# Matmul and batch norm on one core: the first tiles' scale and shift spread without TensorE, and a third chunk of them by columns

## The chip, the cores and the metric

The kernel runs on one core of a Trainium2 chip. The metric is the device time of one execution in microseconds (us); a lower one is better. A core has TensorE (PE; its weight loads are PEld), VectorE (DVE), ScalarE (ACT), GpSimd (POOL) and SyncE (SP), which here issues DMAs alone. Every engine runs its own list of instructions in order and waits for others by semaphores. Matmuls write into PSUM, 8 banks of 128 x 512 float32.

## The reference

```python
y = np.matmul(x, weight)                      # x [16, 512, 1024], weight [1024, 768]
mean = np.mean(y, axis=(0, 1), keepdims=True)
var = np.var(y, axis=(0, 1), keepdims=True)
y_norm = (y - mean) / np.sqrt(var + eps)
return (gamma * y_norm + beta).astype(np.float32)
```

All is float32 outside; the kernel multiplies in bfloat16. Every output column needs the mean and variance over all 8192 rows before its first element can be stored.

## The kernel before

The 8192 rows are 16 chunks of 512 (CH), the 768 columns 6 tiles of 128. GpSimd's DMAs load x (L403) and the weight; VectorE turns x into xT_sb (L428, L435). TensorE then makes y in two forms.

**By columns** (tiles 2 to 5, line L575): the weight stands still, and y comes with columns on the partitions. VectorE takes statistics (L711; for most of tile 2 ScalarE does, L720 and L724), ScalarE keeps y as bfloat16 (L715). Scale and shift are then one value a partition, but the normalized tile must be turned back into rows, by TensorE transposes (L1044), or by SP's DMA transposes (L1220 and L1106).

**By rows** (tiles 0 and 1 together, GA = 2, NA = 256 columns): for chunks 0 to 13 (RC = C - 2 = 14) x stands still (L510), and y comes with rows on the partitions, as it is stored. ScalarE squares (L659), VectorE adds to sums (L662), GpSimd or VectorE adds the squares (L666), ScalarE keeps y (L672). Here scale and shift vary along the free axis, so every partition needs both rows of 256 values. For chunks 14 and 15 these two tiles go by columns instead (`ga_unit`, L814, with statistics in L821 and keeping in L827).

When all chunks are in, `sums_rows` (L871) multiplies the sums with a vector of ones on TensorE, `aggregate_rows` (L887) joins them with the statistics of the column chunks, `root_rows` takes the root, and `scale_rows` and `shift_rows` give scale and shift, a value a partition. `spread_rows` puts them on all partitions: `spread` (L903) multiplies a broadcast column with the float32 identity, once for each tile and for scale and shift, into two PSUM banks; `shift_sbuf` (L915) copies the shift to SBUF for GpSimd.

`rows_out` then writes a row chunk: VectorE multiplies (L937), VectorE (for the k in ADDED) or GpSimd adds the shift (L942), SP stores (L946). `ga_block` writes a column chunk: VectorE normalizes two tiles (L1064), TensorE turns eight blocks (L1074), ScalarE copies (L1082), SP stores (L1085).

`raw_spread` does a spread without TensorE already, for parts of tiles 2 to 4: VectorE copies and transposes in 32 x 32 blocks (L1141, L1142), then copies of 32 partitions gather the values into one row and deal it to the four groups of 32 partitions (L1145), and ScalarE copies them to PSUM (L1158).

The order of all this is not written out. Each piece is a `Task` with a due time, engines with assumed durations, what it depends on and the buffers that it takes. `arrange` (L122) goes through the tasks as a list scheduler and fixes each engine's order from those durations: among the tasks that could begin within 0.2 us (`look`) of the first, the one that is due earliest. So a task that is added or changed can move all that follows on every engine. Transposes can be put between the matmuls of a column unit (`hosts`). `banks`, `rings` and others model PSUM banks and SBUF space.

The last tile (5) ends the kernel: its statistics, `affine` (L1324), norms (L1348), transposes (L1044), copies (L1361) and stores (L1364).

Of the kernel before, what the change touches and what calls it, by code (L numbers as in the profile page):

```python
# [227 lines left out]
def kernel(  # L228
# [19 lines left out]
    P = 128  # L248
    NT = N // P
    KQ = K // 4  # L250
    CH = 512
# [13 lines left out]
    GA = 2  # L265
    NA = GA * P
    GY = 2
    PAD = 50
    HELD = 1
    PAIRED = 1  # L270
    ASTAT = {2:tuple(range(4,16))}
    RC = C - 2
    XT, YB, SQ = C - EARLY, 28, 3
    ADDED = (0,6,16,28,40)
    PARTED, LATE, SINGLE = (4,5,7,8,9,10), (12,13,14,15), (2,3,6)
# [17 lines left out]
    def seq(bi):  # L293

        ins = bi.ins
        prev = last.get(ins.engine)
        if prev is not None:
            tc.add_manual_dep(
                ins, prev,
                mybir.DependencyInfo(mybir.DependencyClass.NoSync, mybir.DependencyReason.DATA),  # L300
                reason="order",
            )
        last[ins.engine] = ins.name
        return bi
# [26 lines left out]
        seq(nc.vector.memset(sums[nt][:, 1:2], float(len(ASTAT[nt]) * CH)))  # L331
    msq = singles.tile([P, GA], f32)
    gst = singles.tile([P, GA, 3 + 12 * (C - RC)], f32)
    seq(nc.vector.memset(gst, float(RC * CH)))
    ngamma = singles.tile([P, NT], f32)
    nscale = singles.tile([P, 1], f32)
# [522 lines left out]


    S = clock[0]
    tot_slot, a0_slot, a1_slot = Slot(banks), Slot(banks), Slot(banks)
    aff = {}

    def sums_rows(eng):
# [24 lines left out]
    def root_rows(eng):  # L890
        seq(nc.scalar.activation(std[:, g], mv[:, g, 1], AF.Sqrt, bias=eps_sb, scale=1.0))

    def scale_rows(eng):
        seq(nc.vector.reciprocal(std[:, g], std[:, g]))
        seq(nc.vector.tensor_mul(scale[:, g], std[:, g], gamma_sb[:, g]))

    def shift_rows(eng):
        seq(nc.vector.tensor_mul(tmp[:, g], mv[:, g, 0], scale[:, g]))
        seq(nc.vector.tensor_sub(shift[:, g], beta_sb[:, g], tmp[:, g]))

    def spread(dst, row, nt):

        seq(nc.tensor.matmul(dst, row[:, nt:nt + 1].to_broadcast([P, P]), ident32, start=True, stop=True,  # L903
                             skip_group_check=True))

    def spread_rows(i):
        def emit(eng):
            a_ps = psum.tile([P, CH], f32, tag="b")
            aff[i] = a_ps[:, 0:NA]
            for a in range(GA):  # L910
                spread(a_ps[:, a * P:(a + 1) * P], (scale, shift)[i], a)
        return emit

    def shift_sbuf(eng):
        seq(nc.scalar.copy(sum1[:, 0:NA], aff[1]))  # L915

    U = S - 30.0
    s1 = task(U, pe(0.9), sums_rows, merges, takes=[tot_slot])
    se = task(U, dve(0.8), sums_entry, [s1], True, uses=[tot_slot])
    ag = [task(U, dve(0.25), aggregate_rows(a), [se] + [h[0] for k, h in ga_half.items() if k[0] == a]) for a in range(GA)]  # L920
    rt = task(U, {"ACT": (0.2, 0.3)}, root_rows, ag)
    sc = task(U, dve(0.3), scale_rows, [rt], True)
    sr = task(U + 0.1, dve(0.35), shift_rows, [sc], True)
    p0 = task(U, pe(0.45), spread_rows(0), [sc], takes=[a0_slot])
    p1 = task(U, pe(0.45), spread_rows(1), [sr], takes=[a1_slot])
    p1.look = 0.6
    sh = task(U, act(0.3), shift_sbuf, [p1], uses=[a1_slot])


    def rows_out(c, s0, s1, k):  # L930
        due = S + 5.0 + 0.62 * k
        n = s1 - s0
        slot = Slot(rings, n * NA)

        def norm(eng):
            slot.o = piece(slot).rearrange("p (s n) -> p s n", n=NA)
            seq(nc.vector.tensor_mul(  # L937
                slot.o, y_row[c].y[:, s0:s1], aff[0][:, None, :].to_broadcast([P, n, NA])))

        def add(eng):  # L940
            row = sum1[:, 0:NA] if eng == "POOL" else aff[1]
# [8 lines left out]
        a = task(due, dve(0.3 * n), norm, [p0] + keeps, takes=[slot], uses=[y_row[c], a0_slot])  # L950
        b = task(due + 0.4, dve(0.3 * n) if k in ADDED else pool(0.59 * n), add, [a, p1 if k in ADDED else sh],
                 uses=[slot, a1_slot] if k in ADDED else [slot])
# [103 lines left out]
    def ga_block(c, due):  # L1056
        yslot = y_row[c]
        slot, bank = Slot(rings, RT * NA), Slot(banks)
        todo = []

        def norm_ga(a):
            def emit(eng):
                part = yslot.y[:, a]
                seq(nc.vector.tensor_scalar(  # L1064
                    part, part, scale[:, a:a + 1], shift[:, a:a + 1], op0=ALU.mult, op1=ALU.add))
            return emit

        def step():
            if not todo:
                o_ps = psum.tile([P, RT, GA, P], bf16, tag="b")  # L1070
                bank.tile = o_ps
                todo.extend((o_ps[:, s, a], yslot.y[:, a, s * P:(s + 1) * P]) for s in range(RT) for a in range(GA))
            dst, src = todo.pop(0)
            seq(nc.tensor.transpose(dst, src, ident))  # L1074

        def emit(eng):
            for _ in range(emit.task.count):
                step()

        def copy(eng):  # L1080
            slot.o = piece(slot).rearrange("p (s n) -> p s n", n=NA)
            seq(nc.scalar.copy(slot.o, bank.tile.rearrange("p s a n -> p s (a n)")))  # L1082

        def store(eng):
            seq(nc.sync.dma_start(out_flat[c * CH:(c + 1) * CH, 0:NA].rearrange("(s p) n -> p s n", p=P), slot.o))  # L1085

        emit.step = step
        norms = [task(due, dve(0.25), norm_ga(a), [sr] + [h[1] for k, h in ga_half.items() if k[1] == c], True, uses=[yslot])
                 for a in range(GA)]
        t = task(due, pe(0.0555 * RT * GA), emit, norms, takes=[bank], uses=[yslot])  # L1090
        emit.task = t
        turns[t] = [RT * GA, RT * GA]
        d = task(due, act(0.905), copy, [t], takes=[slot], uses=[bank])
        task(due, {"SP": (0.38, 0.4)}, store, [d], dma=RT * NA * P * 4 / 1024 / 365.0 * 1.024, uses=[slot])

    for c in range(RC, C):
        ga_block(c, S - 29.8 + 35.5 * (c - RC))

    def raw_turn(nt, c, due):

# [26 lines left out]
    def raw_spread(nt, fin_task):  # L1127
        bank = Slot(banks)
        k = sorted(RAW).index(nt)
        acc, at = ((sum2, 0), (sum2, 2 * P), (sum3, 2 * P))[k]  # L1130
        row = acc[:, at:at + 2 * P].rearrange("p (i n) -> p i n", n=P)
        wide, turned = sum1[:, NA + 64 * k:NA + 64 * (k + 1)], sum3[:, 64 * k:64 * (k + 1)]
# [279 lines left out]
```

## Time and profile before

| | us |
|---|---|
| median of 3 runs (range) | 205.81 (205.71 to 205.83) |
| span of the profiled execution | 204.07 |
| median less span | 1.74 |
| PE busy / DVE / ACT / POOL | 189.3 / 159.3 / 146.2 / 124.1 |
| last matmul of a statistic ends | 186.62 |
| first scaled rows (L937) begin | 107.59 |
| first store of output issued | 109.10 |

For the profiled execution only its span is given; what lies around it is taken from the runs. Times in the profile count from the first instruction. A group's line gives file line, engine, operation, output and inputs with their shapes, count, busy time and mean duration. The chain of work that ended last is followed back from the end, step by step, to what released each piece. In the tables by stretch each engine has its busy time and, in brackets, its instructions; then come the granted clock of TensorE, the DMA engines' busy share and GB/s.

### The profile page before, as it was taken

Reading aid. Unit: us, or ns where it says so; the run is one execution under the profiler, and the core shown is the slowest. Engines: PE = TensorE matmul, PEld = TensorE weight load, DVE = VectorE, ACT = ScalarE, POOL = GpSimd, SP = SyncE. Lnnn points to the kernel's source line nnn. Section 1 sums busy time; section 2 is a strip of 40 time slices with the busy share of each in tenths; the row PEclk is TensorE's granted clock in tenths of the full one; section 3 lists DMA queues with packets and bytes.
Section 4 is the critical chain, followed back from the end, with each engine's and each line's share of the span. In section 5 each row is a group of like instructions: output and inputs, shape, how many; then the busy total and the mean of one; then the engine's idle time right before and its main releaser. Section 6 shows DMA issues by size and latency. Waiting matters only on the chain.

```text
span 204.1 us, 3510 instructions
## 1 busy us (share of the span) xinstructions
PE 189.3 (93%) x1210; PEld 114.5 (56%) x1210; DVE 159.3 (78%) x250; ACT 146.2 (72%) x260; POOL 124.1 (61%) x150
## 2 busy tenths in 40 slices
PE   7969999999999999999999999999999999997900
PEld 3457554657488888777865444444444445544600
DVE  4031879999999999969989998987999878657900
ACT  2001461368989999899978766999998959956950
POOL 7776954877499989997403999389613312940000
PEclk9999999999999999999999999999999999999965
DMA  4999999999999999999686899899999999999998
GB/s 71 172 199 196 176 196 196 196 197 197 190 193 197 197 196 196 196 197 195 103 181 200 297 339 336 248 301 328 295 322 227 336 303 274 347 343 310 310 347 253
DMA packets 98562, 48.74 MB, mean 239 GB/s; under 512 B 24304, under 2 KB 98032, under 8 KB 98544
## 3 DMA queue, kind: packets, MB, share of 16 engines
q0 software_dynamic: 34624, 18.36, 65.5%
q1 hardware_dynamic: 63920, 30.16, 52.6%
q8 instruction: 9, 0.15, 0.3%
q14 instruction: 9, 0.07, 0.1%
HBM read 36.71 MB, written 25.17 MB: 303 GB/s over the span
## 4 chain that ended last, share of the span: by engine, by line
PE 86%; ACT 3%; DMA 3%; POOL 2%; issue 1%; ACTq 0%; DVE 0%; POOLq 0%
PE y_ps L575 54%; PE y_ps L510 24%; PE y_ps L814 4%; ACT o_sb L1361 3%; DMA ring<-in_x_dram 3%; PE o_ps L1044 1%; POOL ring L403 1%; POOL w_sb L387 1%; PE y_ps L753 1%; PE a_ps L903 1%; PE o_ps L1074 0%; ACTq L1407 0%; PE idle_ps L591 0%; PE tot_ps L871 0%; ACT ring L1252 0%
## 5 line engine op out<-in xcount | busy, mean ns | idle before, releaser
L575 PEld LDWEIGHTS <-w_sb 128*128 128x128 bf16 x520 | 50.3, 97 | 57.6
L575 PE MATMUL y_ps<-xT_sb,w_sb 128*128 128x512 bf16 (+1 forms) x272 | 59.3, 371 | 0.0
L575 PE MATMUL y_ps<-x_pl,w_sb 128*128 128x512 bf16 x248 | 57.4, 379 | 0.0
L403 POOL DMA_DIRECT2D ring<-in_x_dram x76 | 47.2, 626 | 14.4 <-DMA ring<-in_x_dram 5.5
L510 PE MATMUL y_ps<-w_sb,xT_sb 128*128 128x256 bf16 x448 | 50.6, 273 | 1.7 <-DMA ring<-in_x_dram 1.6
L510 PEld LDWEIGHTS <-xT_sb 128*128 128x128 bf16 x448 | 43.5, 98 | 9.4 <-DVE xT_sb L435 2.9
L435 DVE STREAM_TRANSPOSE xT_sb<-ring 128x1024 f32<-128x1024 f32 (+1 forms) x29 | 31.2, 1111 | 14.1 <-DMA ring<-in_x_dram 13.9
L711 DVE BATCH_NORM_STATS2 stats<-y_ps 128x6 f32<-128x512 f32 x46 | 30.9, 687 | 7.7 <-PE y_ps L575 7.2
L715 ACT CAST y_sb<-y_ps 128x512 bf16<-128x512 f32 x51 | 29.0, 593 | 10.4 <-DVE stats L711 6.3
L547 ACT COPY x_pl<-xT_sb 128x1024 bf16<-128x1024 bf16 x32 | 32.8, 1063 | 1.7 <-DVE xT_sb L435 1.7
L942 POOL TENSOR_TENSOR ring<-ring,sum 128x1024 f32<-128x1024 f32 (+1 forms) x11 | 23.8, 2188 | 14.9 <-ACT y_ps L724 10.9
L659 ACT ACTIVATE sq_sb<-y_ps 128x512 f32<-128x512 f32 x28 | 16.3, 610 | 16.2 <-PE y_ps L510 15.9
L666 POOL TENSOR_TENSOR sum<-sum,sq_sb 128x512 f32<-128x512 f32 x20 | 25.6, 1278 | 3.0 <-ACT sq_sb L659 1.7
L662 DVE TENSOR_TENSOR sum<-y_ps,sum 128x512 f32<-128x512 f32 x28 | 18.9, 675 | 6.3 <-ACT sq_sb L659 5.3
L672 ACT CAST y_sb<-y_ps 128x512 bf16<-128x512 f32 x28 | 16.3, 594 | 8.2 <-DVE sum L662 8.0
L1178 POOL TENSOR_TENSOR ring<-ring,sum 128x1024 f32<-128x1024 f32 x6 | 14.8, 2477 | 9.8 <-issue 8.5
L937 DVE TENSOR_TENSOR ring<-y_sb,a_ps 128x1024 f32<-128x1024 bf16 (+1 forms) x16 | 16.7, 1079 | 0.1
L1044 PE MATMUL o_ps<-ident,y_sb 128*128 128x128 bf16 x104 | 13.1, 221 | 1.6 <-DVE y_sb L1348 1.5
L1232 ACT CAST ring<-ring 128x1024 f32<-128x1024 bf16 x13 | 13.8, 1063 | 0.6 <-DMA ring<-y_sb 0.6
L1145 POOL COPY sum<-sum 32x256 f32<-32x256 f32 (+1 forms) x17 | 5.8, 340 | 13.4 <-DVE sum L1142 6.5
L428 DVE STREAM_TRANSPOSE xT_sb<-ring 128x2048 bf16<-128x2048 bf16 x6 | 13.5, 2290 | 0.1
L591 PE MATMUL idle_ps<-idle_sb 128*128 128x512 f32 x18 | 9.6, 688 | 1.5 <-DVE idle_sb L316 1.5
(104 smaller groups left out, 153.7 us busy)
## 6 DMA issues: line engine op xcount, KB each, us to landing
out_dram<-ring SPq DMA_DIRECT2D x37, 512.0 KB, 3.4
ring<-in_x_dram POOLq DMA_DIRECT2D x52, 256.0 KB, 8.8
out_dram<-o_sb SPq DMA_DIRECT2D x6, 512.0 KB, 4.7
ring<-in_x_dram POOLq DMA_DIRECT2D x16, 128.0 KB, 5.9
w_sb<-in_weight_dram POOLq DMA_DIRECT2D x8, 192.0 KB, 6.2
out_dram<-ring SPq DMA_DIRECT2D x6, 256.0 KB, 3.0
ring<-in_x_dram POOLq DMA_DIRECT2D x4, 192.0 KB, 7.8
out_dram<-o_sb SPq DMA_DIRECT2D x3, 256.0 KB, 2.5
```

The costliest lines, as they stand in the source:

```text
L403: bi = seq(nc.gpsimd.dma_start(x_bf[32 * i:32 * i + 32], src[:, :, KQ * i:KQ * (i + 1)]))
L435: seq(nc.vector.transpose(dst, src[:, :, jw0:jw1]))
L510: seq(nc.tensor.matmul(y_ps[:, s], x_of(c, jw, e, t * P, (t + 1) * P), w_sb[:, jw, e, 0:NA], start=(s == 0 and jw == 0 and e == 0), stop=( ...
L547: seq(nc.scalar.copy(dst, pairs) if eng == "ACT" else ENG[eng].tensor_copy(dst, pairs))
L575: seq(nc.tensor.matmul(y_ps, w_sb[:, jw, e, nt * P:(nt + 1) * P], moving(c, jw, e, q0 * QR, q1 * QR, parted), start=(jw == 0 and e == 0 an ...
L659: seq(nc.scalar.activation(sq_sb[:, 0:n], slot.tile[:, 0:n], AF.Square))
L662: seq(nc.vector.tensor_add(sum1, slot.tile[:, 0:n], sum1))
L666: seq(ENG[eng].tensor_add(acc, acc, state["sq"][:, 0:n]))
L711: seq(nc.vector.bn_stats(dst, slot.tile))
L715: seq(nc.scalar.copy(y(nt, c), slot.tile))
L937: seq(nc.vector.tensor_mul(slot.o, y_row[c].y[:, s0:s1], aff[0][:, None, :].to_broadcast([P, n, NA])))
L942: seq(ENG[eng].tensor_add(slot.o, slot.o, row[:, None, :].to_broadcast([P, n, NA])))
```

## The change

1. RC becomes C - 3: 13 chunks of tiles 0 and 1 by rows, and chunks 13, 14 and 15 by columns.
2. The spread of scale and shift: `scale_rows`, `shift_rows`, `spread_rows` and `shift_sbuf` go. VectorE writes scale and shift 32 wide (`affine_rows`), transposes them in blocks, ScalarE gathers them into the first 32 partitions of sum1, GpSimd or ScalarE deal them to the other groups of 32, and ScalarE copies the whole 128x512 to one PSUM bank. GpSimd prepares gamma, zero and beta as terms.
3. All three column blocks are due just behind the spread (before, the second was due 35.5 us later), and their copy out of PSUM may go to VectorE.
4. Scratch for `raw_spread` moves from the second half of sum1 to its first; PAD, the unused room in `stats`, goes from 50 to 44.

```diff
-    PAD = 50
+    PAD = 44
...
-    RC = C - 2
+    RC = C - 3
...
-    tot_slot, a0_slot, a1_slot = Slot(banks), Slot(banks), Slot(banks)
+    tot_slot, aff_slot = Slot(banks), Slot(banks)
...
+    wide_rows = sum2[:, 0:2 * GA * 32].rearrange("p (a i n) -> p a i n", i=2, n=32)
+    turned_rows = sum3[:, 0:2 * GA * 32].rearrange("p (a i n) -> p a i n", i=2, n=32)
...
+    def first_rows(eng):
+        seq(nc.vector.scalar_tensor_tensor(
+            gcoef[:, :, 1], mv[:, g, 0], -1.0, gamma_sb[:, g], op0=ALU.mult, op1=ALU.mult))
+
+    def affine_rows(eng):
         seq(nc.vector.reciprocal(std[:, g], std[:, g]))
-        seq(nc.vector.tensor_mul(scale[:, g], std[:, g], gamma_sb[:, g]))
...
+        for a in range(GA):
+            seq(nc.vector.scalar_tensor_tensor(
+                wide_rows[:, a], gcoef[:, a, :, None].to_broadcast([P, 2, 32]), std[:, a:a + 1],
+                gbase[:, a, :, None].to_broadcast([P, 2, 32]), op0=ALU.mult, op1=ALU.add))
...
+    def turn_affine(eng):
+        seq(nc.vector.transpose(sum3[:, 0:2 * GA * 32], sum2[:, 0:2 * GA * 32]))
...
+    def gather_affine(eng):
+        row = sum1.rearrange("p (i a n) -> p i a n", a=GA, n=P)
+        for i in range(4):
+            move_affine(eng, row[0:32, :, :, quad(i)], turned_rows[quad(i)])
+
+    def deal_affine(i):
         def emit(eng):
-            a_ps = psum.tile([P, CH], f32, tag="b")
-            aff[i] = a_ps[:, 0:NA]
-            for a in range(GA):
-                spread(a_ps[:, a * P:(a + 1) * P], (scale, shift)[i], a)
+            move_affine(eng, sum1[quad(i)], sum1[0:32])
         return emit
...
-    sc = task(U, dve(0.3), scale_rows, [rt], True)
-    sr = task(U + 0.1, dve(0.35), shift_rows, [sc], True)
-    p0 = task(U, pe(0.45), spread_rows(0), [sc], takes=[a0_slot])
-    p1 = task(U, pe(0.45), spread_rows(1), [sr], takes=[a1_slot])
-    p1.look = 0.6
-    sh = task(U, act(0.3), shift_sbuf, [p1], uses=[a1_slot])
+    te = task(S - 20.0, pool(0.5), terms_rows, [affine_loads])
+    ft = task(U, dve(0.15), first_rows, ag, True)
+    sr = task(U, dve(0.6), affine_rows, [rt, ft, te] + merges, True)
+    tr = task(U, dve(0.25), turn_affine, [sr], True)
+    gt = task(U, {"ACT": (0.9, 1.0)}, gather_affine, [tr])
+    dl = [task(U + 0.05 * i, {"POOL": (0.6, 0.65), "ACT": (0.6, 0.7)}, deal_affine(i), [gt]) for i in range(1, 4)]
+    p0 = task(U, act(0.6), keep_affine, dl, takes=[aff_slot])
...
-        d = task(due, act(0.905), copy, [t], takes=[slot], uses=[bank])
+        d = task(due, {"ACT": (0.905, 1.0), "DVE": (1.1, 1.2)}, copy, [t], takes=[slot], uses=[bank])
...
-        ga_block(c, S - 29.8 + 35.5 * (c - RC))
+        ga_block(c, S - 29.9 + 0.1 * (c - RC))
```

More of the change, by code (lines that the diff above doesn't have):

```diff
@@ L333 @@
     gst = singles.tile([P, GA, 3 + 12 * (C - RC)], f32)
+    gcoef = singles.tile([P, GA, 2], f32)
+    gbase = singles.tile([P, GA, 2], f32)
     seq(nc.vector.memset(gst, float(RC * CH)))
@@ L891, in root_rows @@
         seq(nc.scalar.activation(std[:, g], mv[:, g, 1], AF.Sqrt, bias=eps_sb, scale=1.0))
-    def scale_rows(eng):
-        seq(nc.vector.reciprocal(std[:, g], std[:, g]))
-        seq(nc.vector.tensor_mul(scale[:, g], std[:, g], gamma_sb[:, g]))
[L897 to L904, printed above, removed]
@@ L906, in spread_rows, with terms_rows @@
-    def spread_rows(i):
+    wide_rows = sum2[:, 0:2 * GA * 32].rearrange("p (a i n) -> p a i n", i=2, n=32)
+    turned_rows = sum3[:, 0:2 * GA * 32].rearrange("p (a i n) -> p a i n", i=2, n=32)
+    def terms_rows(eng):
+        seq(nc.gpsimd.tensor_copy(gcoef[:, :, 0], gamma_sb[:, g]))
+        seq(nc.gpsimd.memset(gbase[:, :, 0], 0.0))
+        seq(nc.gpsimd.tensor_copy(gbase[:, :, 1], beta_sb[:, g]))
+    def first_rows(eng):
+        seq(nc.vector.scalar_tensor_tensor(
+            gcoef[:, :, 1], mv[:, g, 0], -1.0, gamma_sb[:, g], op0=ALU.mult, op1=ALU.mult))
@@ new lines, in affine_rows, with quad @@
+    def affine_rows(eng):
+        seq(nc.vector.reciprocal(std[:, g], std[:, g]))
+        for a in range(GA):
+            seq(nc.vector.scalar_tensor_tensor(
+                wide_rows[:, a], gcoef[:, a, :, None].to_broadcast([P, 2, 32]), std[:, a:a + 1],
+                gbase[:, a, :, None].to_broadcast([P, 2, 32]), op0=ALU.mult, op1=ALU.add))
+    def quad(i):
+        return slice(32 * i, 32 * i + 32)
+    def turn_affine(eng):
+        seq(nc.vector.transpose(sum3[:, 0:2 * GA * 32], sum2[:, 0:2 * GA * 32]))
@@ L907, in emit, with move_affine @@
+    def move_affine(eng, dst, src):
+        seq(nc.scalar.copy(dst, src) if eng == "ACT" else ENG[eng].tensor_copy(dst, src))
+    def gather_affine(eng):
+        row = sum1.rearrange("p (i a n) -> p a i n", a=GA, n=P)
+        for i in range(4):
+            move_affine(eng, row[0:32, :, :, quad(i)], turned_rows[quad(i)])
+    def deal_affine(i):
         def emit(eng):
-            a_ps = psum.tile([P, CH], f32, tag="b")
-            aff[i] = a_ps[:, 0:NA]
-            for a in range(GA):
-                spread(a_ps[:, a * P:(a + 1) * P], (scale, shift)[i], a)
@@ L912, in spread_rows, with keep_affine @@
-        return emit
-    def shift_sbuf(eng):
-        seq(nc.scalar.copy(sum1[:, 0:NA], aff[1]))
+            move_affine(eng, sum1[quad(i)], sum1[0:32])
+        return emit
+    def keep_affine(eng):
+        a_ps = psum.tile([P, CH], f32, tag="b")
+        if eng == "ACT":
+            seq(nc.scalar.copy(a_ps, sum1))
+        else:
+            seq(nc.vector.tensor_copy(a_ps, sum1))
+        aff[0], aff[1] = a_ps[:, 0:NA], a_ps[:, NA:2 * NA]
     U = S - 30.0
@@ L940, in add @@
         def add(eng):
-            row = sum1[:, 0:NA] if eng == "POOL" else aff[1]
+            row = sum1[:, NA:2 * NA] if eng == "POOL" else aff[1]
             seq(ENG[eng].tensor_add(slot.o, slot.o, row[:, None, :].to_broadcast([P, n, NA])))
@@ L949, in rows_out @@
         keeps = [row_end[k][3] for k in row_end if k[0] == c]
-        a = task(due, dve(0.3 * n), norm, [p0] + keeps, takes=[slot], uses=[y_row[c], a0_slot])
-        b = task(due + 0.4, dve(0.3 * n) if k in ADDED else pool(0.59 * n), add, [a, p1 if k in ADDED else sh],
-                 uses=[slot, a1_slot] if k in ADDED else [slot])
+        a = task(due, dve(0.3 * n), norm, [p0] + keeps, takes=[slot], uses=[y_row[c], aff_slot])
+        b = task(due + 0.4, dve(0.3 * n) if k in ADDED else pool(0.59 * n), add, [a, p0] if k in ADDED else [a] + dl,
+                 uses=[slot, aff_slot] if k in ADDED else [slot])
         task(due + 1.0, {"SP": (0.38, 0.4)}, store, [b], dma=n * NA * P * 4 / 1024 / 365.0 * 1.024,
@@ L1064, in emit @@
                 seq(nc.vector.tensor_scalar(
-                    part, part, scale[:, a:a + 1], shift[:, a:a + 1], op0=ALU.mult, op1=ALU.add))
+                    part, part, wide_rows[:, a, 0, 0:1], wide_rows[:, a, 1, 0:1], op0=ALU.mult, op1=ALU.add))
             return emit
@@ L1081, in copy @@
             slot.o = piece(slot).rearrange("p (s n) -> p s n", n=NA)
-            seq(nc.scalar.copy(slot.o, bank.tile.rearrange("p s a n -> p s (a n)")))
+            part = bank.tile.rearrange("p s a n -> p s (a n)")
+            seq(nc.scalar.copy(slot.o, part) if eng == "ACT" else nc.vector.tensor_copy(slot.o, part))
         def store(eng):
@@ L1131, in raw_spread @@
         row = acc[:, at:at + 2 * P].rearrange("p (i n) -> p i n", n=P)
-        wide, turned = sum1[:, NA + 64 * k:NA + 64 * (k + 1)], sum3[:, 64 * k:64 * (k + 1)]
+        wide, turned = sum1[:, 64 * k:64 * (k + 1)], sum3[:, 64 * k:64 * (k + 1)]
         both = turned.rearrange("p (i n) -> p i n", n=32)
```

## The prediction

> **What bounds the kernel now.** I read the busy shares first, then the chain of work that ended last, then the tail in stretches of time. The page:
>
> ```profile
> span 204.1 us, 3510 instructions
> ...
> PE 189.3 (93%) x1210; PEld 114.5 (56%) x1210; DVE 159.3 (78%) x250; ACT 146.2 (72%) x260; POOL 124.1 (61%) x150
> ...
> PE 86%; ACT 3%; DMA 3%; POOL 2%; issue 1%; ACTq 0%; DVE 0%; POOLq 0%
> ```
>
> TensorE holds 86% of the chain. The chain in order of time (start, duration, what) shows why, around the place that the change touches:
>
> ```profile
> 91.22 3.49 PE y_ps L510 x32
> 94.72 2.16 PE y_ps L575 x10
> 96.87 2.72 PE y_ps L814 x24
> 99.60 0.78 PE tot_ps L871 x8
> 100.38 4.56 PE y_ps L814 x40
> 104.94 1.73 PE y_ps L575 x8
> 106.66 1.05 PE a_ps L903 x8
> 107.72 0.51 PE o_ps L1074 x8
> 108.23 1.73 PE y_ps L575 x8
> 109.95 0.45 PE o_ps L1074 x8
> 110.40 58.94 PE y_ps L575 x269
> ```
>
> Each piece begins where the one before it ends. From 12.14 to the last statistic's matmul at 186.62 TensorE has only some 0.1 us of holes, and its matmuls run at full pace (58.94 us / 269 is 219 ns for 512 columns, beside 216 ns in the best stretch, 6.91 / 32). So the end of TensorE's list is the sum of its instructions: what is put in or taken out there moves 186.62 one for one, if nothing new makes it wait.
>
> The rest, 204.07 - 186.62 = 17.45 us, is the tail: statistics of the last tile, its transposes, its stores. In stretches (busy per engine, then clock, DMA share, GB/s):
>
> ```profile
> 172.00:173.00 1.00, 1.00 (x10) 0.53 (x8) 1.00 (x2) 1.00 (x3) 0.00 (x0) 1.00 0.36 101
> 173.00:187.00 14.00, 14.00 (x92) 7.71 (x90) 9.08 (x15) 9.66 (x16) 7.07 (x3) 1.00 1.15 346
> 187.00:192.00 5.00, 3.44 (x42) 2.25 (x40) 4.69 (x18) 4.49 (x10) 0.00 (x0) 1.00 0.91 272
> 192.00:202.00 10.00, 2.09 (x27) 1.35 (x24) 1.64 (x6) 4.67 (x6) 0.00 (x0) 0.68 1.15 347
> ```
>
> From 192 on the stores run at 347 GB/s and set the end; the last tile's 4.19 MB take 12.1 us at that rate, counted from the first of these stores, which TensorE's end releases. Before that the DMA has a hole: 5 us x (347 - 272) / 347 = 1.08 us between 187 and 192, and 0.71 us at 172. That is the slack of the stores: if all earlier ones came up to 1.08 us later, the last tile's would not be held up. So TensorE is the bound, with the store stream 1.08 us behind it.
>
> **The change on TensorE.** (1) Four spreads go: the eight L903 records, 1.05 us of the chain. (2) Chunk 13 goes from rows to columns. A row chunk is 32 matmuls of L510, 3.49 us; a column chunk is 32 of L814: (2.72 + 4.56) / 2 = 3.64 us. That is +0.15. (3) A column chunk must be turned back: eight transposes of L1074, 0.51 and 0.45 us in the two blocks shown; the first held about 0.06 of waiting, so +0.47. The summing matmuls of L871 stay. Sum: -1.05 + 0.15 + 0.47 = **-0.43 us**. Bounds: -0.39 with 0.51 for the block, -0.45 with 0.45. No matmul is left open; all forms stand in the trace.
>
> **The change on the other engines.** The row chunk dropped costs ScalarE 2 x 610 + 2 x 594 = 2.41 us, VectorE 2 x 675 (add to the sums) and one L937 of 1.21, GpSimd 2 x 1278 (squares) and one L942 of 2.39. The column chunk costs VectorE 4 x 423 + 2 x 409 = 2.51, ScalarE 4 x 373 + 1.02 = 2.51. So VectorE and ScalarE break even, GpSimd is rid of 4.95 us, and SP issues the same 512 KB. All of this lies beside TensorE, which has filler from the next tiles' columns.
>
> The new spread is a chain that TensorE does not see. After the root (ended at 106.05) came, before, four small VectorE operations and the matmuls, and the first scaled rows (L937) began at 107.59. Now: reciprocal 0.17; two scalar_tensor_tensor of 128x64, which the trace does not show: between 0.21 (L997, 128x1) and 0.57 (L795, 128x256), I take 0.25 each, nearest to L1141's 0.17 to 0.18 on 128x32; a transpose of 128x128, between 0.245 (128x64) and 0.68 (128x512), on that line 0.31. With gaps this ends at 107.1. The gather is four ScalarE copies of 32x128: between 242 ns (32x64) and 378 ns (128x256), 0.30 with its step, so 1.2 and up to 0.6 if ScalarE is inside a statistic: 108.4. The deal is three copies of 32x512: GpSimd takes 228 ns for 64 and 390 for 256 undisturbed, so 0.61; ScalarE 0.59 (128x512 cast). In parallel two deep, 1.25: 109.7. The copy to PSUM is 0.6: **110.4**. The row output starts 2.8 us late; bounds 2.2 (no wait for ScalarE) and 4.5 (all deals on one engine, and VectorE in the way).
>
> [...] Nine GpSimd copies of 32x256 (L1145) took 390 ns, but 657 and 566 ns where VectorE ran the bf16 norm of L1026 beside them. [...]
>
> What covers the 2.8 us: three column blocks instead of two are now ready ahead of the rows. Norms 0.73 a pair (106.87 to 107.60 in the trace), so VectorE ends them at about 107.8, 108.5 and 109.3; then turn, copy (1.02) and store. Stores of 3 x 0.52 = 1.57 MB go out by about 113; before, 2.1 MB had gone out by 116, and with the first row halves the new kernel should stand at the same. VectorE is 94% busy from 112 to 141 and GpSimd 83%; each has one row chunk less (1.21, 2.39 us). So the last row store, issued at 141.17, moves by about 2.8 - 1.2 = +1.6 (VectorE) or +0.4 (GpSimd), inside the slack of 0.71 + 1.08 = 1.79. Cost: nothing. If that cover is gone, what is late next is the store stream.
>
> ScalarE gets gather, deal, keep and a copy, less L915: some 3 us around 107 to 111, which its idle share from 105 to 125 (about a fifth) takes back; the statistics of tile 2 that it delays hold PSUM banks, but one bank for both rows replaces two. The terms on GpSimd run while it is idle (it waited 10.85 us before its first add).
>
> **Sum.** Span 204.07 - 0.43 = 203.64. The median of the runs shown is 205.81, 1.74 over the profiled span; with the same 1.74 the forecast is **205.38 us**. What a measurement of this kernel can tell from no change is about 0.2%, 0.41 us: the forecast lies on that edge.
>
> **Rivals.**
>
> (a) TensorE waits, 0.12. Its list is in order, and three blocks of transposes now wait for norms, at 107.8, 108.5 and 109.3. The list is written by a planner that gives a norm 0.25 us; a pair measured 0.73, so its third block may stand up to 0.7 us too early. Against it: the two blocks of before waited 0.06 at most. Price: 0.4, so 205.8.
>
> (b) The store stream becomes the bound, slower than before, 0.28. Place: first row outputs after 107.59. If they come L late, and VectorE gives back only 1.21, the stream falls behind by L - 1.21; it decides from L = 1.21 + 1.79 = 3.0 us on, if the column stores cover nothing. [...] For it: the 94% of VectorE, and DMA share above 1.15 in most of 136 to 187. Against it: the early stores, and holes at 172 and 187 to 192.
>
> (c) A little more, 0.12. GpSimd, 4.95 us lighter, adds its rows earlier, the backlog before 187 shrinks, and the tail's first stores (2.11 us to land for 128 KB) find no queue: -0.2 more, 205.2.
>
> The forecast itself has 0.48, from 205.1 to 205.6; as it lies at the edge, I count 0.30 as faster and 0.18 as the same. Faster: 0.30 + 0.12 = 0.42. Same: 0.18 + 0.09 of (a) + 0.01 of (b) = 0.28. Slower: 0.03 + 0.27 = 0.30. The range runs from 205.0 (c with its error) to 206.8 (b), which leaves out half of (b) and a little of (c).
>
> **What would show it.** No float32 matmul after the sums; L814's form 96 times, at 3.64 us a chunk; eight more transposes; TensorE's last statistic at about 186.2 with holes as small as now. First scaled rows at about 110.4 with a store issued by 109. The hole of 187 to 192 is still there: if it is gone and DMA runs at 347 from 173 to the end, (b) is right. If TensorE's pieces between 105 and 112 have gaps ended by VectorE's norms, (a). It would be wrong if the planner's new order, which is dealt out anew for everything behind 97 us, put some other work late; no row here can price that.

## The result and the profile after

The changed kernel takes **209.16 us** (median of 4 runs, 208.46 to 209.63). The kernel before took 205.78 beside it, so the ratio is 1.0161, with a 95% interval from 1.0134 to 1.0189. It is slower by 3.4 us, and the time lies above the range of the prediction. The profiled execution took 208.7 us, 1.8 of it outside the span. It is one of the two shorter of the four, so what follows explains its 2.83 us of span and not the whole 3.4 between the medians.

The page of the kernel after, its lines for span, busy time and the chain of work that ended last:

```profile
span 206.9 us, 3505 instructions
...
PE 189.3 (91%) x1210; PEld 114.0 (55%) x1210; DVE 161.7 (78%) x255; ACT 147.2 (71%) x266; POOL 120.2 (58%) x151
...
DVE 7%; ACT 5%; DMA 3%; issue 2%; POOL 2%; ACTq 0%; PE 0%; DVEq 0%
```

TensorE is as busy as before, but it has gone from the chain: 86% before, 0% now. The chain hops between VectorE, ScalarE, GpSimd and stores. Its pieces near the end show how (start, duration, what):

```profile
175.02 2.37 POOL ring L1204
...
177.41 5.96 DMA out_dram<-ring
...
183.46 1.22 DVE ring L1200
184.69 0.61 DVE stats L713
...
186.05 0.62 DVE fin L713
...
188.47 0.23 DVE fss L1350
...
188.73 0.36 DVE y_sb L1374
```

A store waits 5.96 us until it has landed; only then is its buffer free for VectorE's L1200, and behind that in VectorE's list stand the last statistics. In the kernel before it was TensorE that ended last here.

The stretches of the tail (busy per engine, then clock, DMA share, GB/s) answer to those shown of before:

```profile
172.00:173.00 1.00, 1.00 (x10) 0.53 (x8) 0.95 (x2) 1.00 (x2) 0.40 (x1) 1.00 1.14 344
173.00:187.00 14.00, 14.00 (x89) 7.61 (x88) 9.25 (x14) 10.48 (x16) 6.96 (x3) 1.00 1.16 341
187.00:192.00 5.00, 3.42 (x43) 2.25 (x41) 4.50 (x16) 4.49 (x11) 0.15 (x1) 1.00 1.15 347
192.00:202.00 10.00, 2.63 (x33) 1.77 (x32) 2.18 (x7) 5.21 (x7) 0.00 (x0) 0.86 1.15 346
```

Both holes of the store stream are gone: 344 instead of 101 GB/s at 172, 347 instead of 272 between 187 and 192. The DMA moves 341 to 347 GB/s in every stretch from 172 to 202. That is the sign which the prediction named for its rival (b).

**Where the 2.83 us of span come from** (204.07 to 206.90), from the two traces:

| step | before | after | change |
|---|---|---|---|
| TensorE's list at 155 us, same piece | 155.07 | 154.63 | -0.44 |
| TensorE's wait at 163 | none | 0.96 by the spacing of starts | +0.96 |
| last statistic's matmul ends | 186.62 | 187.14 | +0.52 |
| first store of the last tile is issued | 189.31 | 190.13 | +0.82, so 0.30 of its own |
| that store lands after | 2.11 | 4.12 | +2.01 |
| last store lands | 203.15 | 205.98 | +2.83 |

Of TensorE's 0.44 us, 0.18 stood there before the change reaches its list: the piece behind row chunk 12, the same in both, begins at 88.72 instead of 88.90. From there to 155 the list is 0.26 us shorter.

The 2.01 us of queue ahead of the last tile's stores are the largest term. The queue is a backlog. MB moved by SP's DMAs (stores and DMA transposes) up to a time, summed from the trace, here with three experiments told below:

| by | before | after | e13 | e12 |
|---|---|---|---|---|
| 120 | 4.65 | 3.94 | 3.42 | 4.54 |
| 140 | 10.60 | 10.21 | 9.55 | 10.99 |
| 160 | 16.41 | 15.93 | 15.22 | 16.33 |
| 170 | 19.54 | 18.56 | 18.34 | 19.28 |
| 180 | 22.71 | 21.80 | 21.62 | 22.24 |
| 190 | 25.91 | 25.23 | 25.04 | 25.56 |

The 0.68 MB missing at 190 are 0.68 / 0.347 = 1.96 us at 347 GB/s, close to the 2.01 us of queue. The lag is not simply carried along: 0.71 MB are missing at 120, 0.39 at 140 and 0.98 at 170, so part of it is made good and part is made anew after 160.

The lag begins at the new spread. Lines picked from the timeline of the kernel after (start, duration, engine, what):

```profile
105.51 0.48 DVE L910 SCALAR_TENSOR_TENSOR sum<-gcoef,std,gbase 128x64 f32<-128x64 f32 x2
106.10 0.31 DVE L918 STREAM_TRANSPOSE sum<-sum 128x128 f32<-128x128 f32 x1
106.34 1.34 DVE L1089 TENSOR_SCALAR y_sb<-y_sb,sum 128x512 bf16<-128x512 bf16 x4
106.45 2.50 ACT L921 COPY sum<-sum 32x128 f32<-32x128 f32 x6
107.42 1.06 PE L1099 MATMUL o_ps<-ident,y_sb 128*128 128x128 bf16 x16
107.78 0.61 POOL L921 COPY sum<-sum 32x512 f32<-32x512 f32 x1 [11.93 <-issue]
108.07 2.36 DVE L1108 CAST ring<-o_ps 128x1024 f32<-128x1024 bf16 x2 [0.39 <-PE o_ps L1099]
109.03 0.59 ACT L936 COPY a_ps<-sum 128x512 f32<-128x512 f32 x1
...
110.34 0.73 DVE L1089 TENSOR_SCALAR y_sb<-y_sb,sum 128x512 bf16<-128x512 bf16 x2
110.91 0.79 PE L1099 MATMUL o_ps<-ident,y_sb 128*128 128x128 bf16 x8
...
111.06 0.68 DVE L962 TENSOR_TENSOR ring<-y_sb,a_ps 128x512 f32<-128x512 bf16 x1
111.73 1.22 DVE L1108 CAST ring<-o_ps 128x1024 f32<-128x1024 bf16 x1
112.87 0.68 DVE L967 TENSOR_TENSOR ring<-ring,a_ps 128x512 f32<-128x512 f32 x1
```

The coefficients are in PSUM at 109.03 + 0.59 = 109.62, 2.03 later than the first scaled rows of before. But VectorE is inside the second of two copies of column blocks (L1108, 2.36 us for both), the norms of the third block (0.73) come next, and it begins the first scaled rows at 111.06, 1.44 later still: 3.47 in all. The third copy stands ahead of its first add, which follows at 112.87, and the first row store is issued at 113.58 (before 109.10). GpSimd's first add begins at 114.32 (before 110.46). The copies delay TensorE a little too: the third block's transposes wait for its norms and take 0.62 us to the next piece at 111.53, where the first two blocks take 0.45 each.

The rest of the loss on TensorE stands in its own timeline:

```profile
154.63 1.97 PE L577 MATMUL y_ps<-xT_sb,w_sb 128*128 128x512 bf16 x8
156.44 5.77 PE L577 MATMUL y_ps<-x_pl,w_sb 128*128 128x512 bf16 x26
163.01 3.18 PE L577 MATMUL y_ps<-x_pl,w_sb 128*128 128x512 bf16 x14 [0.80 <-ACT x_pl L549]
```

Up to 155 TensorE is 0.44 us ahead. At 163 it waits for ScalarE's copy of x (L549) for tile 4. In the planner's assumed times this copy is ready only 0.06 us before its use, where the kernel before had 4.8 us or more, because the order behind 97 us is dealt out anew. ScalarE comes to it late:

```profile
157.67 0.38 ACT L1184 COPY a_ps<-sum 128x256 f32<-128x256 f32 x1 [1.15 <-POOL sum L1171]
...
161.92 1.04 ACT L549 COPY x_pl<-xT_sb 128x1024 bf16<-128x1024 bf16 x1
```

So three suspects stood at the start of the experiments: the **late rows** (spread, and copies on VectorE), the **newly dealt order** at 163, and the **backlog of stores** as what carries either to the end.

### The profile page after: what moved, and what is told of

Read it like the earlier page. It is cut to its first block, busy times and chain, and to the rows that moved or that the text cites. A ratio compares the mean times of both kernels' runs of the same rounds, so it can differ in the third digit from the quotient of the medians.

```text
span 206.9 us, 3505 instructions
## 1 busy us (share of the span) xinstructions
PE 189.3 (91%) x1210; PEld 114.0 (55%) x1210; DVE 161.7 (78%) x255; ACT 147.2 (71%) x266; POOL 120.2 (58%) x151
## 5 line engine op out<-in xcount | busy, mean ns | idle before, releaser
L512 PE MATMUL y_ps<-w_sb,xT_sb 128*128 128x256 bf16 x416 | 46.9, 273 | 1.5 <-DMA ring<-in_x_dram 1.3
L512 PEld LDWEIGHTS <-xT_sb 128*128 128x128 bf16 x416 | 40.4, 98 | 8.7 <-DVE xT_sb L437 2.6
L549 ACT COPY x_pl<-xT_sb 128x1024 bf16<-128x1024 bf16 x34 | 34.8, 1055 | 3.1 <-DVE xT_sb L437 1.7
L713 DVE BATCH_NORM_STATS2 stats<-y_ps 128x6 f32<-128x512 f32 x46 | 29.8, 680 | 4.9 <-PE y_ps L577 4.9
L717 ACT CAST y_sb<-y_ps 128x512 bf16<-128x512 f32 x51 | 28.5, 590 | 4.2 <-DVE stats L713 2.6
L967 POOL TENSOR_TENSOR ring<-ring,sum 128x1024 f32<-128x1024 f32 (+1 forms) x10 | 21.4, 2173 | 10.4 <-DVE ring L962 10.3
L668 POOL TENSOR_TENSOR sum<-sum,sq_sb 128x512 f32<-128x512 f32 x18 | 23.0, 1280 | 3.1 <-ACT sq_sb L661 2.5
L664 DVE TENSOR_TENSOR sum<-y_ps,sum 128x512 f32<-128x512 f32 x26 | 17.5, 674 | 6.2 <-ACT sq_sb L661 5.3
L674 ACT CAST y_sb<-y_ps 128x512 bf16<-128x512 f32 x26 | 15.1, 602 | 7.9 <-DVE sum L664 7.8
L962 DVE TENSOR_TENSOR ring<-y_sb,a_ps 128x1024 f32<-128x1024 bf16 (+1 forms) x15 | 15.5, 1069 | 1.6 <-DMA out_dram<-ring 1.6
L1258 ACT CAST ring<-ring 128x1024 f32<-128x1024 bf16 x13 | 13.7, 1050 | 0.1
L816 PE MATMUL y_ps<-xT_sb,w_sb 128*128 128x256 bf16 x96 | 11.4, 275 | 0.0
```

The lines of the kernel that those rows point to most:

```text
L512: seq(nc.tensor.matmul(y_ps[:, s], x_of(c, jw, e, t * P, (t + 1) * P), w_sb[:, jw, e, 0:NA], start=(s == 0 and jw == 0 and e == 0), stop=( ...
L549: seq(nc.scalar.copy(dst, pairs) if eng == "ACT" else ENG[eng].tensor_copy(dst, pairs))
L664: seq(nc.vector.tensor_add(sum1, slot.tile[:, 0:n], sum1))
L668: seq(ENG[eng].tensor_add(acc, acc, state["sq"][:, 0:n]))
L713: seq(nc.vector.bn_stats(dst, slot.tile))
L717: seq(nc.scalar.copy(y(nt, c), slot.tile))
```

## The experiments

Each ratio is against the kernel before on the same chip (206.35, 205.88, 206.03 and 205.85 us in the four groups), with its 95% interval. "After" or "before" says which kernel was edited.

**e1: after, column copies on ScalarE alone.**

```diff
-        d = task(due, {"ACT": (0.905, 1.0), "DVE": (1.1, 1.2)}, copy, [t], takes=[slot], uses=[bank])
+        d = task(due, act(0.905), copy, [t], takes=[slot], uses=[bank])
```

> The changed kernel, but the three column blocks of the first two tiles are copied out of PSUM by ScalarE alone; in the changed kernel the planner gave all three to VectorE (3.6 us of it between 108.1 and 113.0, ahead of the row outputs). Theory A (the row outputs come late, the store stream that feeds on them stays behind and is busy to the end): the first scaled rows begin about 1 us earlier than at 111.06, the lag of 0.71 MB at 120 us shrinks to about 0.4 MB, and the time falls by about 1 us, to 208. Theory B (the order behind 140 us was dealt anew and has bad places of its own, a hole in the stores from 158 to 162 and a wait of TensorE at 162): the time changes with the new order in either direction, with no tie to the lag at 120 us.

Measured: 208.55 us, ratio 1.0105 (1.0067 to 1.0144). TensorE no longer waits at 163. The rows begin at 111.53, but this execution was late from the loads on: the piece behind row chunk 12 begins at 89.78, 1.06 later than in the changed kernel, so counted from there the rows come 0.6 us earlier. VectorE now stands idle for the keep of the coefficients: ScalarE begins their gather at 108.12, behind a statistic, GpSimd ends the last deal at 110.69, and the keep begins at 110.90, behind a column copy:

```profile
111.53 0.69 DVE L962 TENSOR_TENSOR ring<-y_sb,a_ps 128x512 f32<-128x512 bf16 x1 [1.97 <-ACT a_ps L936]
```

By 140 the DMAs are nearly level with before (10.49 MB), then SP, whose list is in order too, stands 3.2 us at a store that waits for ScalarE's L1258, and the lag is back at 150. So the copies on VectorE can be a part, not the whole.

**e2 and e3: each half of the change alone.** e2 is after with `RC = C - 2`, the old due times of the column blocks, copies on ScalarE and PAD 50. e3 is before with `RC = C - 3`, the new due times and PAD 44.

```diff
--- e2, against after
-    PAD = 44
+    PAD = 50
-    RC = C - 3
+    RC = C - 2
...
-        ga_block(c, S - 29.9 + 0.1 * (c - RC))
+        ga_block(c, S - 29.8 + 35.5 * (c - RC))
```

> One part alone: the new spread, with 14 chunks by rows and two by columns, these due and copied as before the change. TensorE has 1.05 us less than before. Theory A: the row outputs start some 3 us late with one column store less to cover it and one row chunk more behind it, so this is at least as slow as the changed kernel: 209 to 210. Theory B: between 204.7 (before less 1.05) and 210, as its order falls out.

> The other part alone: 13 chunks by rows, three by columns and stored first, with the old spread on TensorE. TensorE has 0.62 us more than before. Theory A: the row outputs start at about 108.5 with three column stores around them, the store stream is not behind, and the time is that of TensorE: 206.4. Theory B: 205 to 209.

Measured: 210.08 (1.0200, 1.0157 to 1.0242) and 209.63 (1.0163, 1.0131 to 1.0195). Both halves cost more than expected, together more than the whole. The traces show why they can't be read: the last stores run at 292 and 281 GB/s instead of 347. What had moved is the SBUF address of the buffers that they read, by +64 and -64 bytes, through PAD.

**e5: before, with the buffer 64 bytes on.** To test that, only this line is changed; the order of work stays.

```diff
-    PAD = 50
+    PAD = 53
```

> The kernel before with PAD = 53 instead of 50 and nothing else: the planned order is the same, instruction by instruction, and the buffers that the last tile's stores read (xtpool) begin 64 bytes further on, at 66624 instead of 66560 bytes of each partition, which is no longer a multiple of 512. The two runs of one part alone had shifted them by 64 bytes too (66624 and 66496), and their stores of the last tile went at 281 to 292 GB/s instead of 346. If the address is the cause: the stores from 192 us on fall to about 285 GB/s and the time rises by 2 to 2.5 us, to 208. If it is the chip or the new order: no change, 205.8.

Measured: 208.53, 1.0115 (1.0083 to 1.0147). The last 10 us of stores:

```profile
192.00:202.00 10.00, 2.44 (x32) 1.58 (x28) 1.99 (x7) 5.02 (x6) 0.00 (x0) 0.72 0.95 282
```

282 GB/s where the kernel before has 347. So the address alone costs over 1%. The change itself keeps it: 44 in place of 50 leaves the buffer at byte 66560, a multiple of 512.

**e6 and e7: the two halves again, at that address** (e2 with PAD 48, e3 with PAD 46).

> The new spread alone again, with PAD = 48, which puts these buffers back to 66560. If the address cost 2.2 us of e2_spread_alone, the last stores run at 346 GB/s and the time is about 207.9; what is left over the kernel before, some 2 us, is then the late row outputs (theory A) or the new order (theory B). Without an effect of the address: 210 again.

> Three column chunks alone again, old spread, with PAD = 46, which puts the buffers back to 66560. TensorE's sum says 0.62 us more than before: 206.4 to 206.9 if the address cost the 2.2 to 2.5 us of e3_three_columns_alone, 209.6 otherwise.

Measured: the spread alone 209.06, 1.0147 (1.0107 to 1.0186); the columns alone 207.36, 1.0064 (1.0044 to 1.0084). In e6 the last statistic ends at 185.61, 1.0 us earlier than before, as four spreads less should give, and the kernel is still 1.5% slower: rows begin at 110.62, and 3.76 instead of 4.65 MB have moved by 120. So the spread is the costly half, and its cost isn't TensorE's. In e7 the profiled execution started about 0.9 us late at the loads; less that, its last statistic (188.60) ends 1.1 later than before, not the 0.62 of the sum. In part that is the second and the third block of transposes, each of which waits 0.2 us for its norms on VectorE.

**e4: after, with less to store early.** Row chunks 2, 3 and 4 store a quarter.

```diff
+            e = s0 + 1 if c in (2, 3, 4) else s1
...
-                out_flat[m0 + s0 * P:m0 + s1 * P, 0:NA].rearrange("(s p) n -> p s n", p=P), slot.o))
+                out_flat[m0 + s0 * P:m0 + e * P, 0:NA].rearrange("(s p) n -> p s n", p=P), slot.o[:, 0:e - s0]))
```

> The changed kernel with every instruction in its order, but the stores of row chunks 2, 3 and 4 write a quarter of their rows each (128 of 512; the other rows of the output are left out), 1.18 MB or 3.4 us of the DMA less, all issued between 116 and 125 us. Theory A: the stream catches up before 140 us, and the time falls by 2 to 2.8 us, to about 206.3, where TensorE and its wait at 162 us bind. Theory B: the hole in the stores at 158 to 162 us is one of supply, not of the DMA, so what is saved before it is lost there: the time falls by under 0.7 us.

Measured: 208.8, 1.0122 (1.009 to 1.0155). 1.18 MB less around 120, 3.4 us at 347 GB/s, buy about 0.8 us (1.61% to 1.22%, and the two intervals overlap), and at 160 the lag is what it was (14.63 + 1.18 = 15.81 MB). DMA time that is spared there isn't used for later stores, which aren't ready.

**e10: after, with less scaling and adding of rows** (a quarter for chunks 2, 3 and 4; all is stored).

```diff
+            h = 1 if c in (2, 3, 4) else n
             seq(nc.vector.tensor_mul(
-                slot.o, y_row[c].y[:, s0:s1], aff[0][:, None, :].to_broadcast([P, n, NA])))
+                slot.o[:, 0:h], y_row[c].y[:, s0:s0 + h], aff[0][:, None, :].to_broadcast([P, h, NA])))
```

> The changed kernel in its own order, but the scaling and the adding of row chunks 2, 3 and 4 handle a quarter of their rows (the rest of these chunks is left unscaled). That takes 3 x 0.87 us of multiplying and 0.87 us of adding off VectorE and 2 x 1.74 us off GpSimd, between 115 and 127 us; stores are whole, as in the changed kernel. Theory A as put for VectorE: the lag is made up before 140 us and the time falls by 1.5 to 3 us, to 206.3 to 207.7. Theory B: under 0.7 us, as with the short stores of e4_short_early_stores.

Measured: 209.05, 1.0139 (1.012 to 1.0159). The producers catch up (4.31 MB at 120), but SP then stands 3.6 us, to 125.55, at a row store. The add for it (L969, 124.37 to 125.53) comes in VectorE's list behind a joining of tile 2's statistics (L1003), for which VectorE waits 1.96 us for ScalarE. The DMAs are nearly idle from 124 to 126 (94 GB/s), and at 130 the sum is that of the change again, 7.19 MB. Time given back in one place is lost at the next fixed one.

**e8, e12 and e11: other orders.** e8 is after with tile 4's first matmuls due 4 us earlier; e12 joins the edit of e1 with 2 us earlier; e11 is before with another due time for the rows, which changes 182 of 782 places in the order and nothing else.

```diff
-                part_chunk(c, clock[0] + 0.0 + 4.0 * i, {"DVE": (0.63, 0.7), "ACT": (1.05, 1.1)},
+                part_chunk(c, clock[0] - 4.0 + 4.0 * i, {"DVE": (0.63, 0.7), "ACT": (1.05, 1.1)},
--- e11, against before
-            due = S + 5.0 + 0.62 * k
+            due = S + 5.4 + 0.62 * k
```

> The changed kernel with one due time moved: the copies of x for chunks 12 to 15, which tile 4 needs behind 155 us (L549, the last of which TensorE waited for at 162 us), are due 4 us earlier. The plan is the same up to 140 us, so the row outputs are as late as in the changed kernel. Theory B: TensorE's wait of 0.96 us goes, its last statistic ends at about 186.2 and the hole in the stores at 158 to 162 shrinks; the time falls by 1 to 3 us, to 206 to 208. Theory A: the lag of the stores is there as before, and the time stays within 0.7 us of the changed kernel's, 208.5 to 209.5.

> The changed kernel with two repairs: ScalarE alone copies the column blocks (as in e1_scalar_copies) and the copies of x for tile 4 are due 2 us earlier. TensorE's wait at 162 us should be gone in either theory. Theory A: VectorE has 3.6 us less ahead of the rows, so 1 to 2 us under the changed kernel, 207.5. Theory B: 205.5 to 207, as both bad places that the trace showed are gone.

> The kernel before with the due times of the row outputs moved by 0.4 us (S + 5.4 for S + 5.0), which changes no work, but makes the planner deal out a new order: 182 of its 782 pieces stand elsewhere, from 109 us on. It tells what a new order alone is worth. Theory A: within 0.5 us of the kernel before. Theory B: 1 to 3 us slower.

Measured: e8 208.27, 1.0103 (1.0074 to 1.0133); e12 207.62, 1.0070 (1.0048 to 1.0091); e11 206.2, 1.0006 (0.9991 to 1.002). In e8 the wait at 163 is gone and the plan up to 140 is that of the change; the edit, which deals out the order behind 140 anew, is worth some 0.6% of the 1.6. That this is the wait's own price is not shown: the last statistic ends 0.65 earlier than in the change (186.49), yet the last tile's first store is issued no earlier (190.48 and 190.13); it lands sooner, after 3.29 instead of 4.12. With both bad places mended (e12) the last statistic ends at 186.06 and the rows begin at 109.94; less than half of the loss is left. e11 shows that a newly dealt order need not cost anything by itself.

**e9 and e13: before, with VectorE late.** e9 puts six idle fills ahead of the first scaled rows, e13 five ahead of the second.

```diff
+            for _ in range(5 if k == 2 else 0):
+                seq(nc.vector.memset(sum3, 0.0))
             seq(nc.vector.tensor_mul(
```

> The kernel before, in its own order, with six memsets of 128x512 put on VectorE just ahead of its first scaled rows: 6 x 0.485 = 2.9 us of idle work, which makes the row outputs as late as the changed kernel's (first scaled rows at 110.5 instead of 107.6). Nothing else is added or moved. Theory A, now put more closely (what is lost is not time of the DMA but of VectorE: between 105 and 155 us it has hardly any slack, so what comes late there stays late in its list, and the stores of the later tiles with it, until the DMA is left with a queue that it works off to the end): 1.5 to 2.9 us slower, 207.3 to 208.7. Theory B (the new order behind 140 us): under 0.7 us slower.

> The kernel before in its own order, with five idle fills of 128x512 on VectorE put ahead of the second scaled rows (behind the norms of both column blocks, so that TensorE's list has nothing behind them): some 3.1 us in which VectorE does nothing of use at about 110. Nothing of the computation is left out. Theory 'late rows': VectorE, 94% busy from 112 to 141, can't take 3.1 us back, the stores fall behind as in the changed kernel (0.4 to 0.6 MB at 140 to 160), and the time rises by 0.7 to 1.5%, to 207.3 to 209, with TensorE's last statistic within 0.4 us of that of the kernel before. Theory 'order': lateness alone is taken up by the holes of the store stream (1.8 us) and by idle time, and the time stays within 0.3%, below 206.5.

Measured: e9 211.8, 1.0272 (1.0241 to 1.0302), which says little: the norms of the second column block stood behind the fills, and TensorE waited 3.27 us for them. e13 mends that: 208.33, 1.0112 (1.0087 to 1.0138). Its fills took 2.4 us and 0.7 between them. The order is that of before, and nothing of the change is in it; late work on VectorE alone makes the lag (table above), fills the hole of 187 to 192 (347 GB/s instead of 272), and goes on to TensorE, which I had not expected. Its profiled execution, the slowest of its six, was 0.82 us late from the loads on; counted from there, 0.75 to 0.94 MB are missing between 140 and 170, not 1.05 to 1.21. The chain of e13:

```profile
160.38 3.35 DMA out_dram<-ring
163.85 1.22 DVE ring L1176
165.07 0.46 DVE y_sb L1028
...
170.59 0.46 DVE y_sb L1028
171.10 0.23 PE o_ps L1046
```

A store lands late, VectorE's L1176 waits for its buffer, the norms of tile 4 (L1028) stand behind, and TensorE, which needs them for transposes, waits 0.9 us at 171. The last statistic ends at 188.55, which holds the 0.82. The backlog of stores thus comes back to the engines through the buffers.

**e14, e15 and e16: less to store late.** The same two stores of tile 4 write one of their eight parts, 0.92 MB less, in after (e14), in before (e15) and in e12 (e16).

```diff
+            if nt == 4 and c in (8, 10):
+                seq(ENG[eng].dma_start(dst()[:, 0:1], slot.o[:, 0:1]))
+            else:
+                seq(ENG[eng].dma_start(dst(), slot.o))
-            seq(ENG[eng].dma_start(dst(), slot.o))
```

> The changed kernel, with the same order, in which two late stores of tile 4 (its blocks of chunks 8 and 10) write one of their eight parts: 0.92 MB of the output is left out, at about 176 to 186. Theory 'the store stream is the bound at the end': 0.92 MB are 2.6 us at 347 GB/s, so the lag is gone when the last tile's stores come, the first of them lands about 2.1 us after its issue instead of 4.1, and the last landing follows it by the 13.8 us of the kernel before: 190.1 + 13.8 = 203.9 and a time of about 207.0 (+0.5%), which is TensorE's own lateness. Rival: the last tile's own copies or another engine set the end, and the time stays above 208.

> The kernel before with the same 0.92 MB of tile 4 left out, as a control. Theory 'the store stream is the bound only in the changed kernel': here TensorE's end and the last tile's own 4.19 MB set the time, so it falls by 0.4 us at most (205.4 to 205.9). Rival: the stream binds the kernel before just as much, and it falls by 1 us or more.

> The changed kernel with the column copies on ScalarE and tile 4's first matmuls due 2 us earlier (207.62, last statistic at 186.06), with the same 0.92 MB of tile 4 left out. Theory 'TensorE's gain is there, and the lag of the stores swallows it': first store of the last tile at 188.8, last landing 13.8 later at 202.6, time 205.0 to 205.8, at or below the kernel before. Rival: something else than the stores holds the end, and it stays above 206.8.

Measured: e14 206.95, 1.0048 (1.0029 to 1.0067); e15 205.82, 0.9997 (0.9984 to 1.001); e16 206.07, 1.0004 (0.999 to 1.0018). The stretch of 187 to 192, first in e14, then in e15:

```profile
187.00:192.00 5.00, 3.44 (x39) 2.51 (x38) 4.41 (x16) 4.49 (x11) 0.34 (x1) 0.92 0.88 263
```

```profile
187.00:192.00 5.00, 3.43 (x44) 2.25 (x40) 4.69 (x17) 4.24 (x10) 0.00 (x0) 1.00 0.60 182
```

The hole is back in e14, and two thirds of the loss are gone (1.61% to 0.48%); what is left is about the 0.8 us by which the last tile's first store is issued later (190.13 against 189.31), TensorE's wait at 163 with it, and a rest of the queue, for that store still lands after 2.70 and not 2.11. The same cut does nothing for the kernel before: there the stores have slack, and TensorE sets the end. This is the test that decides: **in the changed kernel the store stream is the bound at the end, in the kernel before it isn't.** In e16 the last statistic ends at 185.83 and the last store lands at 202.38, both 1.1 us earlier than in e15 (186.95 and 203.47), but 0.68 of it stands there before the change's place; TensorE's list behind that is 0.44 us shorter up to 152. The median of its runs is level with before, 0.3 us above what I expected, so of TensorE's gain the whole time shows nothing.

## Why the prediction was wrong, point by point

- **What bounds the kernel before: right.** TensorE, with the stores close behind. e15 bears it out: less to store is worth nothing there.
- **TensorE's sum: its prices right, its total met by luck.** -0.43 was forecast and -0.44 stands at 155, but 0.18 of that was there ahead of the change. The change itself gave -0.26, because the third block of transposes waited 0.17 for norms that stood behind the copies on VectorE. Where ScalarE copies and no block waits (e16 against e15), the same stretch is 0.44 shorter, as the sum says. e6 shows the spreads' share alone (about 1.0).
- **The spread's chain: its prices held, its end did not.** Forecast for the coefficients 110.4, measured 109.6, as the root ended 0.85 earlier; from the root on, 4.35 was forecast and 4.42 measured. The two operations of 128x64 that the trace of before did not show took 0.48 together (0.50 taken), the transpose 0.31 (0.31), one copy of the deal 0.61 (0.61). But the first scaled rows began at 111.06, 3.47 instead of 2.8 late. The 2.8 left VectorE out, which only the upper bound of 4.5 named: it was in the second column copy when the coefficients were ready, and had a block's norms behind that, 1.44 us together.
- **The other engines: wrong.** I booked the column block's copies (1.02 each) on ScalarE. The diff allows VectorE, and the planner gave it all three. So VectorE got 3.6 us at the worst place, and ScalarE and VectorE did not break even there.
- **"Cost: nothing": this is the step that failed.** It let the column stores cover the late rows and took the rest from 1.79 us of slack. By 120 the kernel was 0.71 MB behind, 2.0 us at 347 GB/s, by 170 0.98 MB, 2.8 us: more than all the slack there was, and 2.01 us of it stood as queue ahead of the last tile's stores. (VectorE's share from 112 to 141, 94% in that step, is 26.06 / 29 = 90%; 94% holds from 116 to 136.) Nor can all slack be used: the lists of SP and of the producers are in order, and what one place could have given back (e10, e4) was lost at the next fixed one.
- **Rival (b), given 0.28, is what happened**, at its place and past its point: L = 3.47, over the 3.0 from which it was to decide. Its price was too small. The 206.8 of the range is +1.0 us on the 205.81 of before, with TensorE's gain worth nothing; it was 2.01 of queue, and 0.30 that the chain puts down to a late buffer for VectorE, with TensorE 0.52 late instead of early. The +1.0 stands for rows 4.0 late, 1.0 over the 3.0, with GpSimd's deals held up by VectorE's norms; no run shows a hold-up of that size. The trace showed in its place a deal of 0.61, as priced, and 1.44 that VectorE's own list added.
- **Rival (a) happened, but small.** Its third block of transposes waited for its norms as it said, 0.17 us of the 0.4. TensorE's larger wait was elsewhere, 0.96 at 163, by the order dealt out anew. I had named that at the end as what no row could price, and left it outside the range; the edit of e8, which removes it, gains about 0.6%. The planned slack of a copy, 0.06 us, could have been read from the planner's own sums.
- **GpSimd's deals beside VectorE's norms: not put to a test by the change.** The norms on VectorE ended at 107.68, and GpSimd's one deal began at 107.78 and took 0.61, undisturbed. The planner gave the other two to ScalarE. In e12 one deal did run beside a norm: the deal, which began first (107.84 against 107.97), took 687 ns instead of 607, the norm 705 instead of about 406. (Its two deals took 1.33 us and its six norms 2.29; in e1, where the deals begin as the last norm ends, 1.25 and 1.99.) So both took longer there, the deal by 0.08 us and the norm by 0.30, where the prediction's copies of 32x256 had taken 0.27 and 0.18 longer beside a norm. What more deals beside norms would have cost is not shown.

Still open: how the lateness of the rows divides between spread and copies, since the planner moves other work with every edit; and why e12, whose rows are nearly on time and whose DMAs are ahead at 140, falls behind again by 150. Its trace shows SP standing 3.4 us at a store that waits for ScalarE's L1258; that this alone keeps the rest of the loss was not tried. Open too is what made the part of the lag that came after 160.

## What to carry to other kernels

A step that is off the critical path is not free because the bound has slack somewhere behind it: follow its lateness through every in-order list (producer, DMA issuer, buffers) to the last hole, and count only holes in which the late work would be ready. Test which resource binds the end by taking work from it late and early, in both kernels: 0.92 MB less at the end gave 2.2 us back, 1.18 MB less at 120 about 0.8, and neither would have shown anything alone. When an edit moves addresses or a planner's order, price that by itself first, as e5 and e11 do. Before times of two executions are compared, look whether they are level at a place that the edit doesn't touch.

## What the runs showed of the hardware

The rate of the last stores depended on where their source lies in SBUF. From byte 66560, a multiple of 512, they ran at 346 to 347 GB/s (before, after, e6; in e7 at 329, with a DMA share of 1.09 instead of 1.15); from 66624 at 282 (e5) and 292 (e2), from 66496 at 281 (e3). So 64 bytes up and 64 bytes down gave about the same rate. The rows of these stores are 128 float32, 512 bytes. In e5, whose order of work is that of before, the time is 2.65 us longer (208.53 against 205.88). Only these three addresses were run; what makes the difference is not shown.

A stretch with DMA transposes among the stores moved fewer bytes in about the same busy time: from 155 to 165, with three of them, the kernel before had a DMA share of 1.19 and 265 GB/s; from 173 to 187, with none, 1.15 and 346.
